# Hybrid encoder layer on one Trainium2 core: S5 tables set up behind the first input tiles, side lines a little later, row loads from GpSimd's queue, half of the last output blocks split ahead, and a dense copy of V

## The chip, the cores and the metric

The kernel runs on one core of a Trainium2 chip. Six sequencers work side by side and wait for each other through semaphores: PE (TensorE matmuls, with its weight loads shown as PEld), DVE (VectorE), ACT (ScalarE), POOL (GpSimd), and SP (SyncE), which here only issues DMAs. ACT and POOL issue some DMAs too. Each engine takes its instructions strictly in the order in which they stand. The metric is the device time in microseconds (us) of one execution.

## The reference

One layer of a streaming encoder, for 512 tokens of width 2048, all in fp32:

```python
mod = silu(c) @ w_ada + b_ada                        # six rows of 2048
h = layer_norm(x) * (1 + sc_m) + sh_m
u, q, k, v, z, beta, a, gate_s, gate_g = split(h @ w_in)
y_s = s5_mixer(u, ...) @ w_up_ssm                    # 64 groups, 16 channels, 64 states
y_g = gated_deltanet(q, k, v, z, beta, a, ...) @ w_up_gdn   # 8 heads, chunks of 64
y = (sigmoid(gate_s) * y_s + sigmoid(gate_g) * y_g) @ w_out
x = layer_norm(alpha * x + g_m * y, ln1_g, ln1_b)
h = layer_norm(x) * (1 + sc_f) + sh_f
x = layer_norm(alpha * x + g_f * swiglu(h), ln2_g, ln2_b)
```

The S5 mixer first turns its parameters (`lam_re`, `lam_im`, `log_dt`) into powers of a complex decay and an input factor (`fr`, `fi`); these tables don't depend on the tokens.

## The kernel before

**Products.** Every large product is made of three matmuls per 128x512 tile (`mm3`): the fp32 operands are split into a rounded part `hi` and a rest `lo`, and hi·hi, hi·lo and lo·hi are added in PSUM. These are called main matmuls here; there are 12,216 of them. The weights come as blocks of 512 KB (class `Weights`, L933): SP loads a block into one of three `raw` buffers, ACT casts it to `whi`, DVE subtracts to get `wlo`. `run_ahead` splits two blocks ahead of the one in use. A block serves 24 main matmuls in the input, gate and FFN products, and 12 in the w_mix product and in the last FFN output, where the roles are swapped.

**Stages.** 0 to 168 us: layer norm, adaLN (the 33.5 MB of `w_ada` that the first modulation needs pass through here in pieces) and the input tiles `u` of S5. To about 1061 us: the other input products, with the S5 and GDN work (eight batches, eight heads) set between the main matmuls. Then gates and merge to 1469, w_mix to 1683, and the FFN in six groups of eight hidden tiles, the last of four; the last group's output product and the final layer norm end the kernel.

**Order.** Class `Order` (L61 on) holds a model of the engines' clocks. Side work is written as generators ("lines"): `s5_setup`, `s5_line`, GDN's preparation and recurrence, adaLN, layer norm. Behind each main matmul `tick` (L132) gives a line its next step once `line.t + MARGIN` is not above the modelled clock of PE, where `line.t` is the modelled time at which the step's inputs are there. So MARGIN only moves where in each engine's order a step's instructions stand.

**S5.** `s5_setup` (L272) starts ahead of the input tiles: SP loads `lr`, `li`, `dt`; POOL computes exponentials and angles in 64x128 pieces, ACT takes `sn` and `cs`, POOL goes on to `ar`, `ai`, `fr`, `fi`, PE transposes these four into `px_s`, ACT copies them to `PAr`, `Pi`, `Ftab`, and POOL builds the tables. `o.drain(s5s)` forces the rest behind the input tiles. Each of the eight batches (`s5_batch`, L391) builds V on POOL, transposes it on PE into `G` (two ACT copies of 128x512), and uses V as the weights of eight matmuls into `pk`; these read V with a step of eight elements.

**w_mix and the end.** SP issues, beside the weight blocks, the rows of the modulation (`grow`, by `row_to`, L1598), the rows of the layer norm (`gg`, `gs`) and the tiles of `x` (`at<-in_x`). In the last FFN group the output weights are multiplied by the row `g_f` on DVE (`scaled`), so each block is first scaled, then cast and subtracted; there are eight blocks, two for each quarter `q` of the columns. `ws.limit` lets `run_ahead` split three of them; the other five are taken raw and split inside `last_parts` (L1787).

Of the kernel before, what the change touches and what calls it, by code (L numbers as in the profile page):

```python
# [11 lines left out]
F32 = mybir.dt.float32  # L12
# [44 lines left out]
class Order:  # L57
# [6 lines left out]
    MARGIN = 0.4  # L64
# [326 lines left out]
def s5_batch(k, j, prm, d_col):  # L391
# [56 lines left out]
    for half in range(2):  # L448
        pg = k.psum("s5")
        for i in range(4):  # L450
            pe.transpose(pg[:, 128 * i:128 * i + 128], V[:, 4 * half + i].rearrange("p h s -> p (h s)"), k.c(C_ID))
        act.copy(G[:, 4 * half:4 * half + 4].rearrange("p t n -> p (t n)"), pg)
    Kc = k.sm5.tile([128, 15, 16], F32, name="s5Kc", tag="s5Kc")
    pool.memset(Kc[:, 0:7], 0.0)
    for half in range(2):
        pk = k.psum("s5")
        for i in range(4):
            tau = 4 * half + i
            pe.matmul(pk[:, 128 * i:128 * i + 128], lhsT=V[:, :, :, 7 - tau].rearrange("p g h -> p (g h)"),
# [467 lines left out]

GATES_BEFORE = (0, 1, 1, 1, 1, 1, 1, 1)
# [4 lines left out]
class Weights:  # L933


    def __init__(self, k, pool):
        self.k, self.pool = k, pool
        self.specs, self.raw, self.parts, self.names = [], {}, {}, {}
# [17 lines left out]
    def split(self, upto):  # L956
        while self.cut < min(upto, len(self.specs) if self.limit is None else self.limit):
# [5 lines left out]
            if scale is not None:  # L963
                self.scaled(raw, kts, cols, scale)
            hi = self.pool.tile([128, WB], F32R, name="whi", tag="whi")
# [43 lines left out]
def kernel(ctx, tc, x, c, w_ada, b_ada, w_in, lam_re, lam_im, log_dt, b_re, b_im, c_re, c_im,  # L1009
# [73 lines left out]
    for hf in range(2):  # L1083
        for q in range(4):
            for c0 in range(0, 16, 2):
                ws.plan(w_mix[0, 128 * c0:128 * c0 + 256, 512 * q:512 * q + 512], 2, 512)
    groups = [(j0, min(HG, NHT - j0)) for j0 in range(0, NHT, HG)]
    ffn_order = []
    for gi, (j0, ng) in enumerate(groups):
        nh = min(NHALF, ng) if gi == 0 else 0  # L1090
        ffn_order.append([(j, [hf]) for hf in range(2) for j in range(nh)] + [(j, [0, 1]) for j in range(nh, ng)])
        for j, _ in ffn_order[-1]:
            for base in (0, HID):
                plan1(f_in[0, :, base + 128 * (j0 + j):base + 128 * (j0 + j) + 128])
        for q in range(4):
            for c0 in range(0, ng, 2):
                r0 = 128 * (j0 + c0)
                ws.plan(f_out[0, r0:r0 + 256, 512 * q:512 * q + 512], 2, 512, q if gi == len(groups) - 1 else None)
    ws.limit = len(ws.specs) - 5
# [71 lines left out]
    def ada_line(p, col0, pace):  # L1171
# [8 lines left out]
        depth = 3 if pace else 6 if deep else 4  # L1180
# [62 lines left out]
    start, set5 = ExitStack(), ExitStack()  # L1243
    sp = start.enter_context(pool_of(name="start", bufs=1, side="right"))
    s5p = set5.enter_context(pool_of(name="s5set", bufs=1))
# [116 lines left out]
    s5s = o.add(s5_setup(k, s5p, lam_re, lam_im, log_dt))  # L1362
# [32 lines left out]
    o.drain(s5s)  # L1395
    start.close()
    set5.close()
# [32 lines left out]
    k.sm5 = sp5 = sps.enter_context(pool_of(name="sp5", bufs=1))  # L1430
    alias5 = {"g": "X", "y": "S"}
    alias5w = {"G": "W", "H": "V", "R": "W"}
    k.t5 = lambda n: sp5.tile([128, 512], F32, name="s_" + n, tag="s" + alias5.get(n, n), bufs=2 if n == "U" else 1)
    k.t5w = lambda n: sp5.tile([128, 1024], F32, name="s_" + n, tag="s" + alias5w.get(n, n))
# [421 lines left out]
```

## Time and profile before

| | us |
|---|---|
| median of 3 runs | 3168.74 (3167.68 to 3170.12) |
| the profiled execution | 3170.34 |
| its span, first to last instruction | 3168.6 |
| PE busy in it | 3033.4 |
| mean granted TensorE clock | 0.977 of full speed |

A main matmul of 128x512 starts every 0.227 us at the full clock. Its record is longer, since matmuls overlap, so PE's busy time says when PE had work and not how fast it went; for that the granted clock stands beside it. A wait is named by the instruction that waited and by the one whose semaphore came last. Waits of engines other than PE cost time only where PE stands behind them.

### The profile page before, as it was taken

The numbers are of one execution on the slowest core, as the hardware profiler recorded it, in microseconds if no ns is written. First come the engines' busy times: TensorE is split into PE (matmuls) and PEld (weight loads), VectorE is DVE, ScalarE is ACT, GpSimd is POOL, SyncE is SP. The second block draws the span as 40 slices with busy tenths as digits, with TensorE's granted clock in tenths as the row PEclk, the third lists the DMA queues.
The fourth block names the chain that finished last, engine by engine and source line by source line (L and its number), as shares of the span: only waits on it lengthen the run. The fifth ranks groups of instructions, "written<-read, shape, count | busy, mean of one in ns | idle before, by whom it ended". The sixth has DMA issues, their size and how long they took to land.

```text
span 3168.6 us, 40305 instructions
## 1 busy us (share of the span) xinstructions
PE 3033.4 (96%) x15953; PEld 2499.7 (79%) x15953; DVE 1663.2 (52%) x2217; ACT 954.5 (30%) x1378; POOL 782.8 (25%) x832
## 2 busy tenths in 40 slices
PE   5899989989999999999989999999999999999997
PEld 2588878778777878888769998888888888888885
DVE  6647777666554576756687543333333333333337
ACT  3233333333222343323345631222222222222121
POOL 4834655455112255100022102002001100200202
PEclk8899989999999999999999999999999999999998
DMA  9654334333332688656866553333333333333333
GB/s 330 229 148 110 98 87 111 105 105 95 117 109 84 201 288 288 224 188 207 261 225 192 169 170 103 100 97 110 94 99 110 97 100 101 105 95 102 109 101 120
DMA packets 513534, 458.14 MB, mean 145 GB/s; under 512 B 56145, under 2 KB 403633, under 8 KB 513345
## 3 DMA queue, kind: packets, MB, share of 16 engines
q1 hardware_dynamic: 495904, 408.91, 42.4%
q0 software_dynamic: 10240, 33.56, 3.1%
q10 hardware_dynamic: 7200, 13.10, 1.2%
q8 instruction: 125, 2.05, 0.3%
q14 instruction: 65, 0.52, 0.1%
HBM read 435.60 MB, written 19.89 MB: 144 GB/s over the span
## 4 chain that ended last, share of the span: by engine, by line
PE 64%; DMA 4%; DVE 4%; issue 2%; ACT 2%; POOL 1%; SPq 0%; ACTq 0%; DVEq 0%; POOLq 0%
PE pm L211 47%; PE px_fo L211 14%; DMA raw<-in_w_mix_out_dram 2%; PE px_gd L211 2%; DVE wlo L170 1%; ACT whi L170 1%; DVE at L170 1%; DMA w<-in_w_ada_dram 1%; DVE aacc L170 1%; PE px_ada L211 0%; DMA raw<-in_ffn_w_in_dram 0%; PE px_s L211 0%; ACT f L170 0%; DVE bt L170 0%; DMA g_G<-dG 0%
## 5 line engine op out<-in xcount | busy, mean ns | idle before, releaser
L211 PE MATMUL pm<-at,whi 128*128 128x512 f32 (+1 forms) x3744 | 1145.5, 389 | 8.0 <-ACT whi L170 5.0
L170 DVE TENSOR_TENSOR wlo<-raw,whi 128x1024 fp32r<-128x1024 f32 x541 | 683.4, 1265 | 800.6 <-ACT whi L170 789.7
L170 ACT CAST whi<-raw 128x1024 fp32r<-128x1024 f32 x541 | 567.0, 1050 | 1066.4 <-PE pm L211 454.9
L211 PEld LDWEIGHTS pm<-at,whi 128*128 128x128 f32 x3744 | 683.7, 191 | 137.8 <-ACT whi L170 5.4
L211 PE MATMUL pm<-at,wlo 128*128 128x512 f32 (+1 forms) x1872 | 717.3, 383 | 2.6 <-DVE wlo L170 2.5
L211 PE MATMUL pm<-bt,whi 128*128 128x512 f32 (+1 forms) x2464 | 680.3, 362 | 0.0
L211 PEld LDWEIGHTS pm<-bt,whi 128*128 128x128 f32 x2464 | 442.2, 189 | 71.7 <-issue 0.5
L211 PE MATMUL pm<-bt,wlo 128*128 128x512 f32 (+1 forms) x1232 | 446.0, 362 | 1.5 <-DVE wlo L170 1.5
L211 PEld LDWEIGHTS pm<-at,wlo 128*128 128x128 f32 x1872 | 356.5, 190 | 72.9 <-DVE wlo L170 3.5
L170 POOL TENSOR_TENSOR at<-at,ld 128x512 f32<-128x512 f32 x80 | 120.5, 1538 | 1109.8 <-DVE ld L170 1109.8
L211 PE MATMUL px_fo<-whi,bt 128*128 128x512 f32 x960 | 298.8, 389 | 0.0
L211 PEld LDWEIGHTS pm<-bt,wlo 128*128 128x128 f32 x1232 | 232.9, 189 | 37.8 <-DVE wlo L170 2.2
L211 PEld LDWEIGHTS px_fo<-whi,bt 128*128 128x128 f32 x960 | 180.2, 188 | 37.5
L211 PE MATMUL px_fo<-wlo,bt 128*128 128x512 f32 x480 | 186.7, 389 | 0.0
L170 DVE SCALAR_TENSOR_TENSOR aacc<-w,ccol,aacc 128x512 f32<-128x512 f32 x176 | 163.8, 931 | 6.1 <-DMA w<-in_w_ada_dram 5.1
L170 POOL TENSOR_TENSOR rs<-rs,mhalf 128x1 f32<-128x1 f32 (+1 forms) x13 | 11.3, 872 | 453.1 <-DVE rs L170 453.1
L211 PE MATMUL pm<-whi,bt 128*128 128x512 f32 x336 | 112.5, 405 | 9.8 <-DVE at L170 9.8
L211 PE MATMUL px_fo<-whi,at 128*128 128x512 f32 x336 | 108.2, 392 | 2.0 <-ACT whi L170 2.0
L211 PEld LDWEIGHTS px_fo<-wlo,bt 128*128 128x128 f32 x480 | 90.1, 188 | 18.7
L170 DVE SCALAR_TENSOR_TENSOR gs<-gg,pm 128x512 f32<-128x512 f32 x36 | 24.7, 687 | 142.2 <-ACT gg L170 142.2
L170 DVE TENSOR_TENSOR gs<-gs,pm 128x512 f32<-128x512 f32 x36 | 24.7, 687 | 119.9 <-PE pm L211 119.9
L211 PEld LDWEIGHTS pm<-whi,bt 128*128 128x128 f32 x336 | 64.9, 193 | 26.4 <-DVE at L170 11.7
(412 smaller groups left out, 3232.4 us busy)
## 6 DMA issues: line engine op xcount, KB each, us to landing
raw<-in_ffn_w_in_dram SPq DMA_DIRECT2D x208, 512.0 KB, 4.1
raw<-in_w_in_dram SPq DMA_DIRECT2D x146, 512.0 KB, 4.3
raw<-in_ffn_w_out_dram SPq DMA_DIRECT2D x88, 512.0 KB, 3.7
wad<-in_w_ada_dram SPq DMA_DIRECT2D x64, 512.0 KB, 6.3
w<-in_w_ada_dram SPq DMA_DIRECT2D x128, 256.0 KB, 4.2
raw<-in_w_mix_out_dram SPq DMA_DIRECT2D x64, 512.0 KB, 5.3
w<-in_w_ada_dram POOLq DMA_DIRECT2D x91, 256.0 KB, 4.8
gg<-in_w_ada_dram POOLq DMA_DIRECT2D x37, 256.0 KB, 5.2
```

The costliest lines, as they stand in the source:

```text
L170: r = f(*a, **kw)
L211: r = self.e.matmul(out, **kw)
```

## The change

Six parts. (1) MARGIN is 1.0 us in place of 0.4 until the S5 and GDN lines are done, and 0.4 from there. (2) ACT copies V into a dense `Vs` (tile `s_K`) and the `pk` matmuls take their weights from it. (3) `s5_setup` is no line of its own ahead of the input tiles; it runs as the first part of the S5 line behind them, and the paced adaLN line keeps two loads in flight in place of three. (4) The rows and the tiles of `x` are loaded from POOL's queue. (5) In the last FFN group four of the eight output blocks are planned among the input blocks, two behind each of the first two hidden tiles, and split into spare tiles; one block in place of five is taken raw. (6) For this the four rows `g_f` are loaded as the group begins.

```diff
@@ -61,7 +61,7 @@
...
-    MARGIN = 0.4
+    MARGIN = 1.0
@@ -450,13 +450,15 @@
...
+    Vs = k.t5w("K")
+    act.copy(Vs.rearrange("p (s n) -> p s n", s=8), V.rearrange("p g h s -> p s (g h)"))
...
-            pe.matmul(pk[:, 128 * i:128 * i + 128], lhsT=V[:, :, :, 7 - tau].rearrange("p g h -> p (g h)"),
+            pe.matmul(pk[:, 128 * i:128 * i + 128], lhsT=Vs[:, 128 * (7 - tau):128 * (8 - tau)],
@@ -962,6 +967,15 @@
...
                 self.scaled(raw, kts, cols, scale)
+            if i in self.kept:
+                pairs = self.kept[i]()
+                for s, (hi, lo) in enumerate(pairs):
+                    r = raw[:, cols * s:cols * s + cols]
+                    self.k.act.copy(hi, r)
+                    self.k.v.tensor_tensor(out=lo, in0=r, in1=hi.bitcast(F32), op=S)
+                self.parts[i] = tuple(zip(*pairs))
+                self.cut += 1
+                continue
             hi = self.pool.tile([128, WB], F32R, name="whi", tag="whi")
@@ -1084,19 +1098,28 @@
...
+    kept = []
...
+        out_blocks = [(q, c0) for q in range(4) for c0 in range(0, ng, 2)]
+        def plan_out(n, scale=None):
+            for q, c0 in itertools.islice(out_blocks, n):
+                r0 = 128 * (j0 + c0)
+                ws.plan(f_out[0, r0:r0 + 256, 512 * q:512 * q + 512], 2, 512, q if scale else None)
+            del out_blocks[:n]
+        last = gi == len(groups) - 1
...
-        for q in range(4):
-            for c0 in range(0, ng, 2):
-                r0 = 128 * (j0 + c0)
-                ws.plan(f_out[0, r0:r0 + 256, 512 * q:512 * q + 512], 2, 512, q if gi == len(groups) - 1 else None)
-    ws.limit = len(ws.specs) - 5
+            if last and j < EARLY // 2:
+                kept += range(len(ws.specs), len(ws.specs) + 2)
+                plan_out(2, True)
+        plan_out(len(out_blocks), last)
+    ws.limit = len(ws.specs) - 1
@@ -1177,7 +1200,7 @@
...
-        depth = 3 if pace else 6 if deep else 4
+        depth = 2 if pace else 6 if deep else 4
@@ -1240,9 +1263,8 @@
...
-    start, set5 = ExitStack(), ExitStack()
+    start = ExitStack()
...
-    s5p = set5.enter_context(pool_of(name="s5set", bufs=1))
@@ -1359,7 +1381,6 @@
...
     ws.run_ahead()
-    s5s = o.add(s5_setup(k, s5p, lam_re, lam_im, log_dt))
     xnT = []
@@ -1392,9 +1413,7 @@
...
             ws.run_ahead()
-    o.drain(s5s)
     start.close()
-    set5.close()
@@ -1448,7 +1466,14 @@
...
         u_out(upsum[j])
-    s5l = o.add(s5_line(k, (b_re, b_im, c_re, c_im), dcol))
+    def s5_all():
+        with pool_of(name="s5set", bufs=1) as s5p:
+            yield from s5_setup(k, s5p, lam_re, lam_im, log_dt)
+        k.sm5 = sps.enter_context(pool_of(name="sp5", bufs=1))
+        yield from s5_line(k, (b_re, b_im, c_re, c_im), dcol)
+    s5l = o.add(s5_all())
     psb = [None]
@@ -1483,6 +1508,7 @@
...
+        o.MARGIN = 0.4
@@ -1596,7 +1622,7 @@
...
-        ld.dma_start(out=t, in_=bc(src[0:1, 512 * q:512 * q + 512], [128, 512]))
+        pool.dma_start(out=t, in_=bc(src[0:1, 512 * q:512 * q + 512], [128, 512]))
@@ -1639,7 +1665,7 @@
...
-                ld.dma_start(out=r, in_=bc(src[0:1, 512 * q:512 * q + 512], [128, 512]))
+                pool.dma_start(out=r, in_=bc(src[0:1, 512 * q:512 * q + 512], [128, 512]))
@@ -1698,7 +1724,7 @@
...
                         xa[t][q] = at(F32)
-                        ld.dma_start(out=xa[t][q], in_=x[0, 128 * t:128 * t + 128, sl])
+                        pool.dma_start(out=xa[t][q], in_=x[0, 128 * t:128 * t + 128, sl])
                     for i in range(2):
@@ -1762,11 +1788,21 @@
...
-            k.gf_rows = [row_to(t2("ld"), drow[5], q) for q in range(2)]
+            q2 = P2[1]
+            k.gf_rows = [row_to(t, drow[5], q) for q, t in enumerate(
+                (t2("ld"), t2("ld"), t2("grow"), q2.tile([128, 512], F32, name="gf3", tag="gf3", bufs=1)))]
+            spare = gsp[ng:] + [[adp.tile([128, 512], F32R, name="w1", tag="w1", bufs=4) for _ in range(2)] for _ in range(2)]
+            spare += [[adp.tile([128, 512], F32R, name=n, tag=n, bufs=1) for n in ("aacc", "go")],
+                      [q2.tile([128, 512], F32R, name=n, tag=n, bufs=1) for n in ("aacc2", "keep")]]
+            for n, i in enumerate(kept):
+                ws.kept[i] = lambda n=n: spare[2 * n:2 * n + 2]
+            early = []
...
+            if gi == len(groups) - 1 and j < EARLY // 2:
+                early += [ws.next(2, 512) for _ in range(2)]
@@ -1781,16 +1817,19 @@
-    k.gf_rows += [row_to(bt(F32), drow[5], q) for q in range(2, 4)]
     parts = []
...
             his, los = [], []
-            if q > 1:
-                yield k.gf_rows[q]
+            yield k.gf_rows[q]
             for c0 in range(0, ng, 2):
-                if 2 * q + c0 // 2 < 3:
+                n = 2 * q + c0 // 2
+                if n < EARLY:
+                    his += early[n][0]
+                    los += early[n][1]
+                    continue
+                if n < 7:
                     hi, lo = ws.next(2, 512)
```

PE in the first S5 batch before; `px_s<-cst,s_V` are the transposes of V, `px_s<-s5Cs,s_V` the `pk` matmuls, `pm` main matmuls.

```order
319 L211 MATMUL pm<-at,whi 128x512 x2
320 L211 MATMUL pm<-at,wlo 128x512
321 L216 MATMUL px_s_1656<-cst,s_V 128x128 x4
322 L216 MATMUL px_s_1662<-cst,s_V 128x128 x4
323 L211 MATMUL px_s_1670<-s5Cs,s_V 128x128 x4
324 L211 MATMUL pm<-at,whi 128x512 x2
325 L211 MATMUL pm<-at,wlo 128x512
326 L211 MATMUL px_s_1685<-s5Cs,s_V 128x128 x4
327 L211 MATMUL pm<-at,whi 128x512 x2
```

The same place after; `px_gd` is GDN's.

```order
598 L211 MATMUL pm<-at,whi 128x512 x2
599 L211 MATMUL pm<-at,wlo 128x512
600 L216 MATMUL px_s_2476<-cst,s_V 128x128 x4
601 L216 MATMUL px_s_2482<-cst,s_V 128x128 x4
602 L211 MATMUL px_s_2492<-s5Cs,s_K 128x128 x4
603 L211 MATMUL px_gd<-g_X,g_TT 64x64 x8
604 L211 MATMUL px_gd<-g_TT,g_X 64x64 x8
605 L216 MATMUL px_gd<-cst,g_E 128x128 x4
606 L211 MATMUL pm<-at,whi 128x512 x2
607 L211 MATMUL pm<-at,wlo 128x512
608 L211 MATMUL px_s_2541<-s5Cs,s_K 128x128 x4
```

The transposes and the first four `pk` matmuls stand next to each other in both; these four now read the copy. ACT at this place after:

```order
140 L170 COPY s_G<-px_s_2476 128x512
141 L170 COPY s_G<-px_s_2482 128x512
142 L170 COPY s_K<-s_V 128x1024
143 L170 COPY g_MT<-px_gd 128x512
144 L170 COPY s_S<-px_s_2573 64x256 x4
```

The copy `s_K<-s_V` stands behind both copies to `G`, which wait for the transposes.

ACT in the last FFN group before; `gg` is the gate of a hidden tile, `at<-gs` the cast of that tile's finished values, `whi` a weight block, two for each half of a hidden tile.

```order
947 L170 ACTIVATE gg<-pm 128x512
948 L170 CAST whi<-raw 128x1024 x2
949 L170 CAST at<-gs 128x512
950 L170 CAST whi<-raw 128x1024 x2
951 L170 ACTIVATE gg<-pm 128x512
952 L170 CAST whi<-raw 128x1024 x2
953 L170 CAST at<-gs 128x512
954 L170 CAST whi<-raw 128x1024 x2
```

The same place after; `bt`, `w`, `aacc` `<-raw` are casts of the early output blocks.

```order
957 L170 ACTIVATE gg<-pm 128x512
958 L170 CAST bt<-raw 128x512 x4
959 L170 CAST at<-gs 128x512
960 L170 CAST whi<-raw 128x1024 x4
961 L170 ACTIVATE gg<-pm 128x512
962 L170 CAST w_22917<-raw 128x512
963 L170 CAST w_22919<-raw 128x512
964 L170 CAST aacc<-raw 128x512
965 L170 CAST aacc_22923<-raw 128x512
966 L170 CAST at<-gs 128x512
967 L170 CAST whi<-raw 128x1024 x4
```

The two weight blocks that stood between `gg` and `at<-gs` have the early output blocks' casts in their place, and stand behind `at<-gs`.

POOL in the w_mix stage after; before, the DMAs among these rows stood on SP.

```order
682 L170 DMA at<-in_x_dram 128x512
683 L170 TENSOR_TENSOR rs<-rs,mhalf_137 128x1
684 L170 DMA gg<-in_ln_g_dram 128x512
685 L170 DMA gs<-in_ln_b_dram 128x512
686 L170 TENSOR_TENSOR at<-at,gg 128x512
687 L170 TENSOR_TENSOR at<-at,gs 128x512
688 L170 DMA grow<-dgm 128x512
689 L170 DMA at<-in_x_dram 128x512 x2
690 L170 DMA gg<-in_ln_g_dram 128x512
691 L170 DMA gs<-in_ln_b_dram 128x512
692 L170 TENSOR_TENSOR at<-at,gg 128x512
```

POOL's `at<-at,gg` takes a tile that ACT has written, and the loads for later quarters now stand behind it.

## Rows read from the trace of the kernel before

**Rows 1.** The page's part on busy time, and of the chain that ended last the line by engine, tile and line of the program (share of the span).
```profile
PE 3033.4 (96%) x15953; PEld 2499.7 (79%) x15953; DVE 1663.2 (52%) x2217; ACT 954.5 (30%) x1378; POOL 782.8 (25%) x832
...
PE pm L211 47%; PE px_fo L211 14%; DMA raw<-in_w_mix_out_dram 2%; PE px_gd L211 2%; DVE wlo L170 1%; ACT whi L170 1%; DVE at L170 1%; DMA w<-in_w_ada_dram 1%; DVE aacc L170 1%; PE px_ada L211 0%; DMA raw<-in_ffn_w_in_dram 0%; PE px_s L211 0%; ACT f L170 0%; DVE bt L170 0%; DMA g_G<-dG 0%
```
**Rows 2.** Table by stage: stretch in us and its length, then busy us (and instructions) of PE, PEld, DVE, ACT and POOL, the granted TensorE clock, the share of the DMA engines in use, GB/s.
```profile
60.00:88.00 28.00, 25.02 (x111) 16.32 (x110) 16.15 (x14) 9.87 (x15) 24.33 (x47) 0.94 0.95 326
88.00:134.00 46.00, 35.12 (x118) 20.76 (x117) 22.93 (x22) 11.29 (x19) 38.75 (x63) 0.80 0.69 233
134.00:168.00 34.00, 32.29 (x125) 19.92 (x124) 27.44 (x58) 11.40 (x16) 18.40 (x29) 0.90 0.56 186
...
400.00:600.00 200.00, 187.84 (x1340) 155.37 (x1340) 140.31 (x243) 67.13 (x139) 112.07 (x109) 0.95 0.35 95
...
1480.00:1690.00 210.00, 187.48 (x815) 148.93 (x814) 149.98 (x198) 88.27 (x109) 27.61 (x18) 0.96 0.73 235
...
3100.00:3121.00 21.00, 15.84 (x38) 9.60 (x38) 16.04 (x21) 6.74 (x11) 0.00 (x0) 0.67 0.51 177
```
**Rows 3.** Waits of PE in 88 to 134 us: instruction's tile and line, what it waited for, us in total, times, longest.
```profile
PE pm L211 <- ACT whi L170: 5.0, 1, 5.0
PE px_s L216 <- POOL fi L170: 2.6, 1, 2.6
PE pm L211 <- DVE wlo L170: 2.5, 1, 2.5
```
**Rows 4.** Waits of ACT in the same stretch, same columns.
```profile
ACT PAr L170 <- PE px_s L216: 12.5, 1, 12.5
...
ACT sn L170 <- POOL sr L170: 10.0, 1, 10.0
```
**Rows 5.** Timeline of POOL, first and last of the operations that lead from the loaded `dt` to the table entries `fi` (start us, duration us, instruction, idle before it and what ended that).
```profile
57.24 1.29 POOL L170 TENSOR_SCALAR er<-dt 64x1 f32<-64x1 f32 x1 [9.40 <-DMA dt<-in_ssm_log_dt_dram]
...
123.95 0.45 POOL L170 TENSOR_TENSOR fi<-t,den 64x128 f32<-64x128 f32 x1
```
**Rows 6.** Waits of PE in 200 to 1100 us, the first and the last of 14 kinds; over all 14 kinds they come to 37.8 us in 23 waits.
```profile
PE px_s L216 <- POOL s_V L170: 6.7, 4, 3.8
...
PE px_s L211 <- ACT s_G L170: 0.3, 1, 0.3
```
**Rows 7.** Table by stretch (columns as in rows 2) around one wait of PE for POOL `s_V`, which lasted from 724.27 to 726.43 us.
```profile
724.00:727.00 3.00, 0.83 (x6) 0.57 (x5) 2.93 (x3) 0.00 (x0) 2.51 (x2) 0.95 0.54 149
727.00:730.00 3.00, 3.00 (x16) 2.78 (x14) 0.00 (x0) 1.17 (x2) 0.00 (x0) 0.50 0.11 32
730.00:733.00 3.00, 3.00 (x42) 2.85 (x41) 2.05 (x4) 0.00 (x0) 0.00 (x0) 0.98 0.00 0
```
**Rows 8.** The instructions on tile `px_s`, weight loads of two kinds: durations min/median/max in ns, then first and last start.
```profile
L211 PEld LDWEIGHTS px_s<-s5Cs,s_V x128: 312/335/337, 218.0 to 733.3; 128*128 128x128 f32 x128
...
L211 PEld LDWEIGHTS px_s<-s_U,s_K x128: 186/192/192, 269.7 to 778.6; 128*128 128x128 f32 x128
```
**Rows 9.** Timeline of PE in the first of the eight S5 batches (columns as in rows 5, with the count of records; an fp32 matmul leaves two records).
```profile
217.22 1.09 PE L216 MATMUL px_s<-cst,s_V 128*128 128x128 f32 x8
218.15 2.07 PE L211 MATMUL px_s<-s5Cs,s_V 128*128 128x128 f32 x8
...
220.75 1.94 PE L211 MATMUL px_s<-s5Cs,s_V 128*128 128x128 f32 x8
```
**Rows 10.** Groups of ACT instructions in 188 to 1061 us: busy us, mean ns of one, idle before.
```profile
L170 ACT CAST whi<-raw 128x1024 fp32r<-128x1024 f32 x102 | 106.8, 1048 | 178.9 <-PE pm L211 146.3 <-issue 24.3 <-DVE wlo L170 3.1
L170 ACT COPY s_K<-s_R 128x1024 f32<-128x1024 f32 x8 | 17.6, 2201 | 0.1
...
L170 ACT COPY s_G<-px_s 128x512 f32<-128x512 f32 x16 | 8.8, 588 | 35.1 <-PE px_s L216 35.1
```
**Rows 11.** Waits of PE in 1480 to 1800 us.
```profile
PE pm L211 <- DVE wlo L170: 7.0, 9, 1.0
...
PE pm L211 <- ACT whi L170: 1.3, 1, 1.3
```
**Rows 12.** Waits of SP, the queue that issues the loads, in 1480 to 1720 us.
```profile
SPq L170 <- DVE wlo L170: 99.4, 54, 6.1
...
SPq L170 <- DVE bt L170: 6.4, 1, 6.4
```
**Rows 13.** Waits of POOL in the same stretch.
```profile
POOL at L170 <- ACT at L170: 26.9, 3, 14.2
```
**Rows 14.** The page's list of DMA issues, the same load from SP's queue and from POOL's (count, KB each, median us from issue to landing).
```profile
w<-in_w_ada_dram SPq DMA_DIRECT2D x128, 256.0 KB, 4.2
...
w<-in_w_ada_dram POOLq DMA_DIRECT2D x91, 256.0 KB, 4.8
```
**Rows 15.** Timeline around the start of the last output blocks.
```profile
3097.39 0.69 DVE L170 TENSOR_TENSOR gs<-gs,pm 128x512 f32<-128x512 f32 x1 [2.48 <-PE pm L211]
...
3098.11 0.62 ACT L170 CAST bt<-gs 128x512 fp32r<-128x512 f32 x1 [4.46 <-DVE gs L170]
...
3099.37 1.22 DVE L170 TENSOR_TENSOR raw<-raw,ld 128x1024 f32<-128x1024 f32 x1
...
3100.98 1.04 ACT L170 CAST whi<-raw 128x1024 fp32r<-128x1024 f32 x1 [2.25 <-DVE raw L170]
...
3102.08 0.55 PE L211 MATMUL px_fo<-whi,at 128*128 128x512 f32 x1 [2.00 <-ACT whi L170]
```

More of the change, by code (lines that the diff above doesn't have):

```diff
@@ L925 @@
 NHALF = 8
+EARLY = 4
 GATES_BEFORE = (0, 1, 1, 1, 1, 1, 1, 1)
@@ L937, in __init__ @@
         self.k, self.pool = k, pool
-        self.specs, self.raw, self.parts, self.names = [], {}, {}, {}
+        self.specs, self.raw, self.parts, self.names, self.kept = [], {}, {}, {}, {}
         self.used = self.loaded = self.cut = 0
@@ L1429 @@
     k.tc = lambda n: gp.tile([128, 256], F32, name="g_" + n, tag=n, bufs=1 if n == "X" else 2)
-    k.sm5 = sp5 = sps.enter_context(pool_of(name="sp5", bufs=1))
     alias5 = {"g": "X", "y": "S"}
     alias5w = {"G": "W", "H": "V", "R": "W"}
-    k.t5 = lambda n: sp5.tile([128, 512], F32, name="s_" + n, tag="s" + alias5.get(n, n), bufs=2 if n == "U" else 1)
-    k.t5w = lambda n: sp5.tile([128, 1024], F32, name="s_" + n, tag="s" + alias5w.get(n, n))
+    k.t5 = lambda n: k.sm5.tile([128, 512], F32, name="s_" + n, tag="s" + alias5.get(n, n), bufs=2 if n == "U" else 1)
+    k.t5w = lambda n: k.sm5.tile([128, 1024], F32, name="s_" + n, tag="s" + alias5w.get(n, n))
     k.u_done = 0
```

## The prediction

> **What bounds the kernel now.** I read the page's busy times first, then the chain that ended last, the table by stage, and the waits of PE in each stage. PE is busy for 3033.4 of 3168.6 us, and one kind of main matmul alone holds 47% of the chain [rows 1]; none of the six parts removes a main matmul. So the change can only win where PE stood still or ran at a low clock: the start, where PE is busy for 35 of 46 us at a granted clock of 0.80 [rows 2]; the S5 and GDN stage, with 37.8 us of waits [rows 6]; w_mix, with 187 of 210 us busy [rows 2]; and the last output blocks, with 15.8 of 21 us busy at 0.67 [rows 2]. The clock goes with the waits: PE waited 2.16 us until 726.43, from 727 to 730 the granted clock was 0.50, the lower of its two levels (1.2 in place of 2.4 GHz), and after that 0.98 [rows 7]. Half a clock over 3 us is 1.5 us lost, so a wait of over 2 us costs that much more than itself.
>
> **S5 set up behind the input tiles: -17 at the start.** From 88 to 168 us the DMA engines moved 46 us x 233 GB/s + 34 x 186 = 17.0 MB. From 60 to 88 they moved 326 GB/s at 0.95 of their time [rows 2]; at that rate 17.0 MB takes 52 us. If nothing else held these 80 us up, they would end 28 us earlier. That is the largest gain. The smallest is what names POOL's tables directly, the 2.6 us of `px_s <- POOL fi` [rows 3] and 1.5 of clock: about 4. Between lie 5.0 us for `whi` and 2.5 for `wlo` [rows 3], which I put down to ACT: it stood 10.0 us in front of `sn` and 12.5 in front of `PAr` [rows 4], weight casts queued behind both, and both are S5 instructions that go. I take 17, near the middle.
>
> **The same set-up in the middle: +4.** Its POOL operations from `dt` to `fi` took 124.40 - 57.24 = 67 us [rows 5]. After, 291 main matmuls stand between its first instruction and the transposes on PE that need `fi`, 291 x 0.227 = 66 us, in which POOL has GDN's work too and ACT again has `sn`, `cs` and `PAr` in a row with casts. If it just fits, it costs nothing. If ACT is blocked as before, PE loses 5.0 + 2.6 + 2.5 again [rows 3] and two times 1.5 of clock, 13 us. I take 4, nearer to the fit.
>
> **MARGIN: -13.** Each step of a line gets its place 0.6 us later on PE. The 23 waits of rows 6 come to 37.8 us; four or so are under 0.6 us and go whole, and 19 that shrink by about 0.55 us give 10. Those just over 2 us, like the one of rows 7, may then leave the clock up, 1.5 us each; I count two, 3 us. At best, with more falling under it, -20. At worst lines that end later hold their tiles longer and others wait instead: +5.
>
> **Dense V: +21.** A weight load from V takes 335 ns, one from a dense tile 192 [rows 8]. The two groups of four `pk` matmuls took 2.07 and 1.94 us, and eight dense records of the same shape 1.09 [rows 9]: 4.01 - 2.18 = 1.8 us saved in each batch. Against it stands a new wait. The first four `pk` matmuls stand directly behind the eight transposes, which end at 217.22 + 1.09 = 218.3 [rows 9]. They now need ACT's copy of V, which stands behind the two copies to `G`. Those wait for the transposes, the first for four of them (ready at about 217.9), and take 0.59 us each [rows 10], to 219.1. The copy itself isn't in the trace. ACT's dense 128x1024 took 1.05 us; `s_K <- s_R`, 128x1024 with a step of eight elements on one side, took 2.20 [rows 10]. The new copy reads with a step of eight, so it is nearest to the second: it ends at 221.3, PE waits 3.0 us, and loses 1.5 to the clock: 3.0 + 1.5 - 1.8 = 2.7 a batch, 8 x 2.7 = 21 us. At the dense price PE waits 1.9 us and keeps its clock, and the edit costs 8 x 0.1, nothing. It ends at -5 if main matmuls cover part of that, and at +25 if a cast of 1.05 us stands ahead on ACT in half of the batches.
>
> **Row loads from POOL: -7.** In w_mix PE waits 7.0 us for `wlo` and 1.3 for `whi` [rows 11], because blocks land late. SP, which loads them, also waits for tiles that the rows and `x` need, as the 6.4 us for `bt` [rows 12]; 99.4 us are for its own raw buffers, and stay [rows 12]. Without the others the blocks are asked for sooner. I count 7 of these 8.3; at best 12, with the clock; at worst +5, where `x` comes later. What hides a late `x`: it is issued at the third of a quarter's eight blocks and used behind the last, six blocks of 12 x 0.227 = 2.72 us later, 16 us, and a load from POOL's queue lands after 4.8 [rows 14].
>
> This is where the Trainium skill speaks against the change. The row shows 4.8 us from POOL's queue and 4.2 from SP's for one kind of load [rows 14], which is inside the 16 us. "SBUF — State Buffer", in the box on how DVE can hold up DMAs, says that descriptors of a DMA from GpSimd's queue are written by GpSimd, which DVE locks out during some of its operations, and that SP's or ACT's queue is the remedy. The row's 0.6 us doesn't show more than that; by the row the sum stays, by the rule the fourth rival below gains.
>
> **Last output blocks: -3.** In 3100 to 3121 us 38 matmuls took 21 us in place of 38 x 0.227 = 8.6 [rows 2]: 12.4 us lost, since five raw blocks are scaled (1.22), cast (1.04) and subtracted one behind the other [rows 15]. One raw block behind seven ready ones hides, so 12 go. But behind the first two hidden tiles of the group the next weight block's cast now stands behind `at <- gs`, which waits for the tile's own end: `gs` 0.69, the cast 0.62, the block's cast 1.04 [rows 15], and some 0.3 us of passing on, about 2.6, with 1.5 of clock and some 0.4 until `wlo` 4.5, twice 9. If the stall is as in rows 15, 2.00 us, and half of it is covered, the part gives -10; if the early blocks push DVE's `wlo` back too, +2. The rows `g_f` are issued a whole group ahead and hide.
>
> **Sum.** -17 + 4 - 13 + 21 - 7 - 3 = -15. The profiled execution took 3170.3, of which 3168.6 is the span; 3170.3 - 15 = 3155.3. It lay 1.6 us above the median of 3168.74, which gives 3153.7; I say **3154**.
>
> **Rivals.**
> *All gains, V free* (0.27): the copy costs the dense price, and the set-up fits. -17 - 13 + 0 - 7 - 3 = -40, so 3129; with the start at 22 and MARGIN at 18, 3119. For it: ACT is busy for 67 of 200 us in this stage [rows 2]. Against: the only copy of this size with a step took 2.20 [rows 10].
> *The start's loss is moved* (0.20): `fi` comes late and ACT blocks the casts as before, 13 in place of 4; MARGIN gives only its 5 us of small waits. -17 + 13 - 5 + 21 - 7 - 3 = +2, so 3171. For it: 67 us of POOL work against 66 of cover [rows 5]. Against: beside GDN's steps POOL no longer works against the adaLN sums on DVE, which were at work in those 67 us.
> *POOL's queue holds `x` up, slower* (0.13): POOL waits for ACT up to 14.2 us in one place [rows 13], and a load behind that wait is issued that much later. With 16 us of lead and 4.8 to land it begins to cost above 11 us. A lag of 20 us, two such waits in part, costs 9 us in each of four quarters, 36 in place of -7: 3154 + 43 = 3197; with half the quarters 3176. The rule on GpSimd's descriptors would work here. For it: loads now stand between POOL's `at<-at,gg`. Against: for the first two quarters nothing on POOL stands ahead of them.
> *The change as summed* (0.40): 3154, itself from 3140 to 3166.
>
> **Chances.** I call within 0.2% the same, 6.3 us, 3162.4 to 3175.1, about what a measurement of this kernel can tell from no change. Faster: 0.33 of the summed case's 0.40, all of the first rival's 0.27 and 0.05 of the second's, 0.65. Same: 0.07, 0.11 and 0.02 of the third's, 0.20. Slower: 0.04 of the second's and 0.11 of the third's, 0.15. The range takes most of the first rival and the third's low case: 3117 to 3178.
>
> **What would show it.** Start: the 216th main matmul, at 168 us before, near 150, and no wait for `fi` there. Set-up: PE waits for `px_s <- POOL fi` near 250 us of 0 to 4 us. V: eight waits of PE for ACT `s_K` of about 3 us with a granted clock of 0.50 behind; under 2 us each means the dense price. MARGIN: fewer than 19 waits in the stage, V's apart. w_mix: busy time of PE nearer to the stage's length, no PE wait for DVE `at` behind a late `x`. End: two PE waits of about 2.6 us for ACT `whi` in the last group, none over 1 us in the output blocks. The forecast is wrong if the copy of V takes under 1.5 us, if the middle shows waits for POOL's tables of over 5 us, or if w_mix gets longer.

## The result, and the profile after

The changed kernel takes 3131.78 us (median of 4 runs, 3128.48 to 3134.89) against 3168.21 of the kernel before; the ratio is 0.9884, 95% interval 0.9867 to 0.9902, so 36 us or 1.2% faster. The forecast was 3154, 15 us faster. The way was right and the time lay in the range (3117 to 3178), but the gain was 2.4 times the one forecast. The first rival's 3129 hits the time by luck: its reason, that the copy of V is free, is refuted by the runs. The profiled execution has a span of 3129.2 us and a clock of 0.982.

Where the time went is easiest seen between given main matmuls, since their number is the same in both. The starts of the k-th main matmul are counted in the two profiled executions; the table gives the us between them.

| main matmuls | stage | before | after | difference |
|---|---|---|---|---|
| 0 to 216 | input tiles of S5 | 98.4 | 80.3 | -18.1 |
| 216 to 294 | to the old place of the S5 line | 20.6 | 17.7 | -2.9 |
| 294 to 2931 | S5 and GDN | 920.5 | 909.0 | -11.5 |
| 2931 to 4464 | gates, merge | 360.0 | 356.1 | -3.9 |
| 4464 to 5232 | w_mix | 214.2 | 207.6 | -6.6 |
| 5232 to 6000 | first FFN tiles | 103.0 | 108.5 | +5.5 |
| 6000 to 11000 | FFN | 1051.4 | 1052.4 | +1.0 |
| 11000 to 12000 | to the last group | 226.7 | 235.2 | +8.5 |
| 12000 to the end | last outputs, layer norm | 104.0 | 95.0 | -9.0 |

Another 2.3 us lie ahead of the first main matmul, so these two executions differ by 39 us where the medians differ by 36.

The page's busy times after, as in rows 1:

```profile
PE 3003.2 (96%) x15953; PEld 2485.0 (79%) x15953; DVE 1648.4 (53%) x2217; ACT 971.5 (31%) x1386; POOL 814.8 (26%) x904
```

PE is busy for 30 us less, at the same share. The table by stage after, with columns as in rows 2; the last two stretches stand 40 us earlier than in rows 2, as the work does:

```profile
88.00:134.00 46.00, 46.00 (x166) 26.65 (x165) 32.80 (x34) 15.30 (x21) 0.00 (x0) 0.91 0.92 320
134.00:168.00 34.00, 34.00 (x156) 28.17 (x155) 13.28 (x15) 12.66 (x18) 0.00 (x0) 0.95 0.45 137
...
1440.00:1650.00 210.00, 192.64 (x855) 153.96 (x855) 156.90 (x208) 90.29 (x111) 47.48 (x52) 0.97 0.76 247
...
3060.00:3081.00 21.00, 21.00 (x94) 17.29 (x93) 14.64 (x18) 3.86 (x5) 1.15 (x3) 1.00 0.30 104
```

From 88 to 134 us PE is busy throughout at 0.91, and POOL not at all: its tables are gone from there [rows 2, 5]. The DMA engines move 320 GB/s in place of 233, and none of the waits of rows 3 is left. In the last outputs PE is busy for 21 of 21 us at 1.00, in place of 15.84 at 0.67.

Waits of PE from 170 to 1100 us, answering rows 6 (the first, the third and the sixth of ten kinds; the others come to 16.0 us):

```profile
PE px_s L211 <- ACT s_K L170: 21.5, 8, 2.7
...
PE px_s L216 <- POOL s_V L170: 4.8, 3, 2.5
...
PE px_s L216 <- POOL fi L170: 2.2, 1, 2.2
```

The eight waits for V's copy are there, 2.7 us each; that for `fi` in the middle is one of 2.2 us. Without those of `s_K` PE waits 23 us in place of 37.8. One batch, on the timeline, answering rows 9:

```profile
308.08 1.07 ACT L170 COPY s_G<-px_s 128x512 f32<-128x512 f32 x2 [5.14 <-PE px_s L216]
...
309.04 2.05 ACT L170 COPY s_K<-s_V 128x1024 f32<-128x1024 f32 x1
...
311.14 2.08 PE L211 MATMUL px_s<-s5Cs,s_K 128*128 128x128 f32 x8 [2.62 <-ACT s_K L170]
```

and the copy and the matmuls' weight loads by form (columns as in rows 8):

```profile
L211 PEld LDWEIGHTS px_s<-s5Cs,s_K x128: 186/192/338, 311.1 to 868.8; 128*128 128x128 f32 x128
...
L170 ACT COPY s_K<-s_V x8: 2035/2036/2066, 309.0 to 861.4; 128x1024 f32<-128x1024 f32 x8
```

The copy stands behind both `G` copies and takes 2.04 us; PE, done with the transposes at 308.51, waits 2.62. The weight loads fell from 335 to 192 ns, as a dense tile has it [rows 8].

The waits of PE at the end, from 2900 us on:

```profile
PE pm L211 <- ACT whi L170: 4.7, 2, 2.4
PE pm L211 <- DVE wlo L170: 1.1, 2, 0.5
```

Two waits for `whi`, 2.4 us the longer, stand where the early blocks' casts took the place of the next tile's, and the wait for `whi` of rows 15 is gone.

### The profile page after: what moved, and what is told of

Same layout as the page of the kernel before. It is cut to its first block, busy times and chain, and to the rows that moved or that the text cites. A ratio compares the mean times of both kernels' runs of the same rounds, so it can differ in the third digit from the quotient of the medians.

```text
span 3129.2 us, 40248 instructions
## 1 busy us (share of the span) xinstructions
PE 3003.2 (96%) x15953; PEld 2485.0 (79%) x15953; DVE 1648.4 (53%) x2217; ACT 971.5 (31%) x1386; POOL 814.8 (26%) x904
## 4 chain that ended last, share of the span: by engine, by line
PE 81%; POOL 6%; DVE 4%; DMA 3%; ACT 3%; issue 2%; SPq 0%; ACTq 0%; POOLq 0%; DVEq 0%
PE pm L211 57%; PE px_fo L211 15%; PE px_gd L211 3%; PE px_s L211 2%; DMA raw<-in_w_mix_out_dram 2%; DVE wlo L170 1%; PE px_adr L211 1%; ACT whi L170 1%; PE px_u L211 1%; PE px_ada L211 1%; POOL s_V L170 1%; DVE at L170 1%; POOL eq L170 1%; DVE aacc L170 1%; POOL g_E L170 0%
## 5 line engine op out<-in xcount | busy, mean ns | idle before, releaser
L211 PEld LDWEIGHTS px_fo<-whi,bt 128*128 128x128 f32 x960 | 180.2, 188 | 37.4
L170 POOL DMA_DIRECT2D w<-in_w_ada_dram x101 | 55.4, 550 | 91.8 <-DVE aacc L170 65.4
```

What stands on the lines that cost most here:

```text
L170: r = f(*a, **kw)
L211: r = self.e.matmul(out, **kw)
```

## The experiments

All were timed beside the kernel before, which read 3168.2 to 3169.1 throughout. Differences under some 4 us between two changed kernels say little. Up to main matmul 2931 the changed kernel and three of its variants below (loads from SP, the old tail, the early blocks between) have the same instructions in the same order on PE, DVE, ACT and POOL, and their profiled executions took 909.0 to 913.1 us from 294 to 2931.

**Undoing one part at a time.** First the copy of V:

```diff
-    Vs = k.t5w("K")
-    act.copy(Vs.rearrange("p (s n) -> p s n", s=8), V.rearrange("p g h s -> p s (g h)"))
...
-    lhsT=Vs[:, 128 * (7 - tau):128 * (8 - tau)]
+    lhsT=V[:, :, :, 7 - tau].rearrange("p g h -> p (g h)")
```

> The changed kernel with one part undone: the pk matmuls read V itself again and ACT makes no copy. Theory A (the prediction's term): the copy costs 21 us over the eight batches, so without it the time falls from 3132 to about 3111. Theory B (accounts of the trace after: 21.5 us of waits for s_K, about 7 us of half clock behind them, less 15 us of faster matmuls): it costs 13, so about 3119. Rival C: the copy pays, because PE's stops there only take the place of other stops: 3135 or more, with the waits for other engines in the S5 and GDN stage grown by 15 us or more.

It took 3113.75 us, ratio 0.9827 (0.9814 to 0.9841): 18 us faster without the copy. Theory A's 21 is nearest. Between 294 and 2931 9 us went (909.0 to 899.8; up to 13 by the spread just named), the rest in w_mix (4) and the first FFN tiles (7), where only the order differs. Rival C falls.

MARGIN back to 0.4:

```diff
-    MARGIN = 1.0
+    MARGIN = 0.4
```

> The changed kernel with MARGIN 0.4 throughout. Theory A (the prediction's term): MARGIN is worth 13 us, so about 3145. Theory B (accounts of the trace after: waits other than for s_K fell from 38 to 23 us, and half clock behind them by about 6): 21 to 23 us, so about 3154, with the waits in the stage back near 38 us beside s_K's. Rival C: MARGIN is worth nothing and the side work only had to start later: 3132.

3155.79 us, ratio 0.9962 (0.9950 to 0.9975): 24 us slower. The stretch 294 to 2931 rose to 941.3 us with 60 us of stops, 37 of them not for `s_K`. (The profiled execution, 3164 us, is the slowest of five, the others 3152 to 3157, so its stages read high.) Theory B holds, A is too small, C falls.

The S5 set-up at the start again:

```diff
+    s5s = o.add(s5_setup(k, s5p, lam_re, lam_im, log_dt))
     xnT = []
...
+    o.drain(s5s)
     start.close()
...
-        depth = 2 if pace else 6 if deep else 4
+        depth = 3 if pace else 6 if deep else 4
```

> The changed kernel with the S5 set-up back ahead of the input tiles and the paced adaLN line at three loads. Theory B: the start gained 20 us and the set-up in the middle costs one wait of 2.2 us, so about 3150, and the 216th main matmul comes at 168 us in place of 148. Theory A (the prediction's terms): 17 less 4, 3145. Rival C: the start's gain is given back in the middle by lines that begin later: 3132, with the 2931st main matmul 0 to 3 us from where it is now.

3150.84 us, ratio 0.9944 (0.9930 to 0.9957): 19 us slower. 0 to 216 took 99.4 us again, and 294 to 2931 911.2, within 2 us of the changed kernel's. So the start's gain isn't given back; B holds. The run puts back the set-up and the third load in flight together, so what each of them gave isn't told apart.

The loads from SP's queue again:

```diff
-        pool.dma_start(out=t, in_=bc(src[0:1, 512 * q:512 * q + 512], [128, 512]))
+        ld.dma_start(out=t, in_=bc(src[0:1, 512 * q:512 * q + 512], [128, 512]))
```

(and the same for the layer norm's rows and `x`).

> The changed kernel with the rows and the tiles of x loaded from SP's queue again. Theory A (the prediction's term): the loads from POOL are worth 7 us, so about 3139. Theory B (accounts of the trace after): w_mix gained 7 us and the first FFN tiles lost 7, since rows of the layer norm stand behind POOL's waits; together nothing, so 3130 to 3134, with main matmuls 4464 to 5232 about 7 us slower and 5500 to 6000 about 6 us faster than now. Rival C: the first FFN tiles are slower for another reason (the new order): the loss at 5500 to 6000 stays and the time is near 3139.

3126.19 us, ratio 0.9867 (0.9853 to 0.9880): 6 us faster. None of the three theories said this. w_mix fell from 207.6 to 201.6 us and the first FFN tiles stayed slow (109.3), so the loss there has another reason than POOL's queue, and the loads from POOL cost in w_mix what they were to bring. Behind the last matmul, in the final layer norm, another 3 us went (19.6 to 16.7). Both recur: in the seven kernels here with the loads on POOL's queue w_mix took 203.5 to 210.1 us, in the four changed kernels with them on SP's 200.2 to 201.6, and behind the last matmul these four took 16.7 or 16.8. PE's waits for weight blocks in w_mix, in the changed kernel:

```profile
PE pm L211 <- DVE wlo L170: 3.6, 4, 1.3
PE pm L211 <- ACT whi L170: 2.2, 1, 2.2
```

and with SP's queue, where none for `whi` is left:

```profile
PE pm L211 <- DVE wlo L170: 1.5, 3, 0.8
```

These are 4.3 of the 6 us. The first row of ACT's waits there, in the same two kernels:

```profile
ACT whi L170 <- DMA raw<-in_w_mix_out_dram: 64.8, 28, 9.3
```

```profile
ACT whi L170 <- DMA raw<-in_w_mix_out_dram: 53.0, 24, 4.3
```

With the rows on POOL's queue ACT waited up to 9.3 us for one weight block, with them on SP's up to 4.3. The sum of these waits is not the cost: in the kernel with three edits below, with SP's queue, it is 65.1 us, and w_mix takes 200.2.

The old tail:

```diff
-EARLY = 4
+EARLY = 0
...
-    ws.limit = len(ws.specs) - 1
+    ws.limit = len(ws.specs) - 5
```

> The changed kernel with no output block split early and five taken raw, as before. Prediction's terms (12 us gained in the output blocks, 9 lost in front): 3 us slower, 3135. Accounts of the trace after (9 us gained behind main matmul 12000, 8.5 lost from 11000 to 12000): 3132, the same. Rival: the early part is a clear gain or loss of 5 us or more.

3137.24 us, ratio 0.9901 (0.9886 to 0.9916): 5.5 us slower. 11000 to 12000 went back to 226.7 us and the stretch behind to 105.8, so by its own two stretches the early part gains 2.3 us; most of the rest lies between 294 and 2931 (913.1), which this edit doesn't touch. It is a small gain, near the 3 us of the prediction's terms.

**MARGIN alone, in the kernel before.** This was the run that settled the case:

```diff
-    MARGIN = 0.4
+    MARGIN = 1.0
...
         o.drain(gl)
+        o.MARGIN = 0.4
```

> The kernel before with one part alone: MARGIN 1.0 until the S5 and GDN lines are done. Prediction's term: -13, so 3155. Theory (its worth is the 24 us that undoing it cost in the changed kernel): 3144, with the stops of PE between main matmuls 294 and 2931 at 15 to 23 us in place of 37.5. Rival: it is worth that much only beside the copy of V, whose waits it gives room: 3158 to 3165.

3132.25 us, ratio 0.9882 (0.9865 to 0.9898): 37 us faster, as much as the whole change. Every expectation put the gain too low. Three other values followed:

> The kernel before with MARGIN 0.7 until the S5 and GDN lines are done. Theory M (a step that is placed later finds its inputs there; the stops shrink with the margin and so does the half clock behind them): between 0.4 and 1.0, main matmuls 294 to 2931 in 900 to 912 us, stops there 24 to 33 us, time 3145 to 3158. Rival J (each margin gives another order, and the order decides by chance): the stretch lies outside 895 to 918, or the stages with the same margin in both (gates, w_mix, first FFN tiles) differ from before by more than 8 us in sum and make up most of the difference.

> The kernel before with MARGIN 1.6 until the S5 and GDN lines are done. Theory M: most of the 13 stops that are left at 1.0 are chains that are late by over 1 us, so a little more: stops 10 to 17 us, main matmuls 294 to 2931 in 880 to 889 us, time 3122 to 3132. Rival L (steps that wait longer end the lines later and hold tiles, so other waits grow): the stretch is 892 us or more. Rival J (chance of the order): the stretch is near 890 and the later stages decide, by up to 10 us either way.

> The kernel before with MARGIN 0.1 until the S5 and GDN lines are done, 0.4 behind them. Theory M (the steps are placed too early for what DVE, ACT and POOL really take, so an earlier place makes long waits): main matmuls 294 to 2931 take 930 us or more, 9 or more waits of PE of at least 2 us, time 3175 to 3195. Rival J (0.4 happened to give a bad order, and any other margin gives a better one): the stretch at 895 to 912 us, 3145 to 3160. Rival N (the margin matters only up from 0.4): 915 to 925 us and 3163 to 3173.

| MARGIN | us | ratio, 95% interval | 294 to 2931 | PE's stops there | 2931 to 4464 | w_mix | first FFN tiles |
|---|---|---|---|---|---|---|---|
| 0.1 | 3153.25 | 0.9950 (0.9937 to 0.9962) | 921.0 | 37.4 | 355.5 | 207.0 | 102.6 |
| 0.4 (before) | 3168.7 | 1 | 920.5 | 37.5 | 360.0 | 214.2 | 103.0 |
| 0.7 | 3144.22 | 0.9916 (0.9901 to 0.9931) | 899.0 | 26.2 | 356.0 | 210.0 | 105.0 |
| 1.0 | 3132.25 | 0.9882 (0.9865 to 0.9898) | 889.7 | 19.0 | 356.4 | 206.9 | 107.2 |
| 1.6 | 3131.31 | 0.9879 (0.9865 to 0.9894) | 871.5 | 12.3 | 370.0 | 208.5 | 112.2 |

(Stops are waits of PE over 0.2 us, summed.) At 0.7 and 1.6 theory M is right on the stops and, to about 1 us, on the time; the stretch came out shorter than it said. At 0.1 M falls; rival N has the stretch right and rival J the time.

Two effects stand apart. In the S5 and GDN stretch a larger margin helps from 0.4 up, in PE's stops and in the busy time behind them; at 0.1 it is as at 0.4. (At 1.6 some line steps pass into the next stretch; the two together take 1241.5 us, against 1246.1 at 1.0 and 1280.5 at 0.4.) Behind it, where the margin is 0.4 in all five, the kernel before is slower than the others by 4 to 7 us in w_mix and, but for 1.6, by some 4 us in the gates: its order was a poor one there, and the four other margins are rid of it. For 0.1 this is 12 of its 15 us. The waits of PE show where, in the kernel before in the gates and in w_mix:

```profile
PE px_ada L211 <- DVE aacc L170: 2.7, 1, 2.7
```

```profile
PE px_ada L211 <- DVE aacc L170: 4.8, 1, 4.8
```

These are steps of the adaLN line; at 0.1 and 1.0 neither wait is there. The changed kernel at 0.4 has the first again (2.65 us, 360.7 us in the gates), so that one is no accident of a single kernel. The S5 and GDN stretch in the kernel before and at 1.0 (columns as in rows 2):

```profile
188.73:1109.23 920.50, 882.47 (x5896) 729.95 (x5894) 576.99 (x933) 301.69 (x574) 392.65 (x410) 0.97 0.40 114
```

```profile
188.11:1077.83 889.72, 870.39 (x5887) 721.37 (x5886) 563.13 (x921) 296.01 (x568) 380.28 (x395) 0.99 0.40 114
```

PE is busy for 12 us less with the same main matmuls; the granted clock rose from 0.97 to 0.99.

**Mending what cost.** The copy of V ahead of the transposes, with a step between:

```diff
+    Vs = k.t5w("K")
+    act.copy(Vs.rearrange("p (s n) -> p s n", s=8), V.rearrange("p g h s -> p s (g h)"))
     G = k.t5w("G").rearrange("p (t n) -> p t n", t=8)
...
     pool.memset(Kc[:, 0:7], 0.0)
+    yield G
```

> The changed kernel with ACT's copy of V put ahead of the transposes and their two copies, and a step of the line between these and the pk matmuls, so that main matmuls can stand between. Theory B (the wait for the copy is what costs, the dense weights themselves save): the eight waits for s_K go, 21.5 us and about 7 of half clock, so the stretch from main matmul 294 to 2931 falls from 909 to about 880 us and the time to about 3103, below the 3114 without any copy. Rival C (most of what the undone copy gave came from other places that only moved with the planner's order: 9 of 18 us were in that stretch): the stretch falls to 885 to 895 and the time ends between 3105 and 3120. Rival D: ACT now holds weight casts up for the copy's 2.0 us, and PE waits for whi instead: 3125 or more.

3096.84 us, ratio 0.9774 (0.9759 to 0.9788). The stretch took 878.8 us and has no wait for `s_K` left; its table row:

```profile
164.49:1043.28 878.79, 854.04 (x5892) 706.02 (x5890) 560.31 (x947) 310.15 (x576) 444.56 (x523) 0.99 0.40 113
```

B holds: the wait was the cost, and 30 of the 35 us lie in this stretch. Dense weights, with the copy off PE's path, are 17 us better than none. The added step of the line is part of that, since the kernel without a copy hasn't got it; what the step alone would give wasn't run. The prediction's price for the faster weight loads, 1.8 us a batch, accounts for 15.

The early output blocks between the blocks of the second product:

```diff
+                    if u and ws.used in ws.kept:
+                        early.append(ws.next(2, 512))
                     hi, lo = ws.next(8, 128)
```

> The changed kernel with each early output block planned between the blocks of the second product of a hidden tile in place of two behind the tile, so that the next tile's first weight blocks are cast ahead of at<-gs. Theory (the order of ACT's casts makes the stall): the two waits for whi of 2.4 us go, main matmuls 11000 to 12000 take 227 to 228 us in place of 235, and the time falls by 8, to about 3124. Rival (DVE, which now scales and subtracts blocks in between, is what is late): PE waits for wlo instead, the stretch stays at 232 or more and the time at 3130.

3127.37 us, ratio 0.9870 (0.9855 to 0.9884): 4 us faster. 11000 to 12000 took 227.4 us with no wait of PE, as the theory has it; the time fell by half of that. Between 294 and 2931, which the edit doesn't touch, the profiled execution took 912.2 us for 909.0, so the medians can't tell 4 from 8.

**Together.**

> The changed kernel with three edits that each were faster alone: the copy of V first (-35), rows and x from SP's queue (-6), the early output blocks between the blocks of a product (-4). If they add up, 3132 - 45 = 3087; if the order of the later stages decides again by chance, 3080 to 3097. A rival: with V's waits gone SP's queue is fuller in w_mix and the rows cost there again, 3097 or more.

3080.18 us, ratio 0.9722 (0.9708 to 0.9736): 88 us faster than before, 52 than the change. The sum of the three was 3087.

> The same three edits with MARGIN 1.6 in place of 1.0. Theory M: stops between main matmuls 294 and 2931 fall further, by 5 to 10 us with their clock, so 3077 to 3084 if the three edits alone give 3087. Rival L: lines that end later make other waits, 3090 or more.

3082.73, ratio 0.9729 (0.9715 to 0.9742): no gain over 1.0. The stretch took 876.2 us against 878.2, and its stops fell by 2 us and not by 5 to 10, so theory M falls here.

> The best kernel so far (three edits, 3080) with MARGIN kept at 1.0 to the end. Theory M: the lines of the layer norm and of adaLN beside w_mix and the first FFN tiles are placed too early too, their stops of 13.4 and 6.5 us shrink by a third or more, 3066 to 3075. Rival: there the lines are the longer chain, or the stops come from weight blocks, and a later place costs: 3080 or more.

3088.37, ratio 0.9742 (0.9728 to 0.9755): 8 us slower; the rival holds. Behind the S5 and GDN stage setting MARGIN back is right: the three stages there took 5 us more in sum, the first FFN tiles 114.0 us in place of 109.1.

## Why the prediction was right or wrong

| step, as forecast | forecast | by undoing it | else |
|---|---|---|---|
| S5 set up behind the input tiles, with its cost in the middle | -13 | -19 | |
| MARGIN | -13 | -24 | -37 alone |
| dense V | +21 | +18 | |
| row loads from POOL | -7 | +6 | |
| last output blocks | -3 | -5.5 | |

With MARGIN at what it gives alone the parts sum to -19.1 - 36.6 + 18.0 + 5.6 - 5.5 = -37.6, and the change measured -36.4; with the value from undoing it they sum to -25.0. The first sum mixes terms from two kernels, so its fit doesn't prove that the parts add up. By the profiled executions MARGIN gave the S5 and GDN stretch 31 us alone and 32 beside the other parts, and w_mix 7.3 and 2.5; undoing it cost 33 us between these executions and 24 between the medians, so much of the 12 us between 24 and 37 may be the spread of the runs.

**MARGIN is the step that failed.** It said that the 23 waits shrink by up to 0.6 us each, 10 us, with 3 for the clock, and it put the stages behind at nothing. Of the 21 us that the forecast missed, this term is 11 by undoing it and 24 by MARGIN alone; the next largest, the row loads, missed 13 the other way. In the stretch alone it gave 31: PE's stops fell by 18.5 and its busy time by 12. The working took each wait for a lateness that a shift shortens by at most the shift. Redone wait by wait from the trace of the kernel before, where eight of the 23 waits are under 0.6 us and not four, that gives at most 11.6 us for 0.6 and 6.5 for 0.3; the runs gave 18.5 at 1.0 and 11.3 at 0.7. At 0.1 the stops come to the same as at 0.4. So the waits aren't the old ones less the shift; each margin makes another set:

| MARGIN | stops of 2 us or more | us | shorter stops | us |
|---|---|---|---|---|
| 0.1 | 5 | 20.0 | 21 | 17.3 |
| 0.4 (before) | 9 | 29.1 | 12 | 8.4 |
| 0.7 | 2 | 5.8 | 21 | 20.3 |
| 1.0 | 5 | 12.7 | 10 | 6.3 |
| 1.6 | 2 | 6.9 | 5 | 5.4 |

From 0.4 to 1.0, 16.4 of the 18.5 us are of the long stops. The busy time fell with them, as the granted clock rose from 0.97 to 0.99. None of the three signs of being wrong that the prediction named appeared, and its sign for MARGIN, fewer than 19 waits beside V's, came true with 12: it counted waits and could not show a gain that was too small. One long stop followed back shows how several queues make it. Here is the longest, in the kernel before (columns as in rows 5):

```profile
668.46 2.49 POOL L170 TENSOR_TENSOR s_W<-PAi,s5Cs 128x1024 f32<-128x1024 f32 x1
...
668.99 2.44 DVE L170 TENSOR_TENSOR s_K<-s_S,tab81s 128x448 f32<-128x448 f32 x1
...
671.02 2.66 POOL L170 TENSOR_TENSOR s_H<-s_H,s_W 128x1024 f32<-128x1024 f32 x1
...
671.46 4.32 DVE L170 TENSOR_TENSOR s_S<-s_S,s_K 128x448 f32<-128x448 f32 x2
...
678.02 1.22 DVE L170 TENSOR_TENSOR wlo<-raw,whi 128x1024 fp32r<-128x1024 f32 x1
679.15 0.69 DVE L170 TENSOR_TENSOR g_v<-g_v,ro 128x512 f32<-128x512 f32 x1
...
679.98 1.09 PE L216 MATMUL px_gd<-cst,g_v 128*128 128x128 f32 x4 [5.19 <-DVE g_v L170]
```

PE waited 5.19 us for `g_v`, which stood on DVE behind S5's steps and a `wlo`. One of those steps took 2.44 us beside POOL's `s_W`, the next two 4.32 us together beside its `s_H` and GDN's `g_G`; the planner's model counts 0.67 us for each (0.2 + 448 x 0.00105, in `Engine`). At 1.0 there is no wait of PE for `g_v` in the stretch. The margin doesn't take such growth away: summed over the stretch, DVE's instructions took 105 us more in the kernel before than each at its fastest (the shortest of the same instruction and shape in the five kernels of the first table of margins), and 101 us more at 1.0. That fits a margin that leaves room for work which takes longer than the model has it. It is argued from this stop; the other stops were not followed.

Another 11 us of MARGIN weren't in the working at all: 3.6 in the gates and 7.3 in w_mix, where the margin didn't change. The table of margins shows that the order before was a poor one there. The first FFN tiles gave 4 back, where PE's waits for ACT `ld` rose from 2.4 to 7.2 us.

**The start** was sized about right, 17 forecast and 21 seen to matmul 294, and nothing was given back in the middle, where I had put 4: one wait of 2.2 us, after which the clock stayed up. On POOL the way from `dt` to `fi` took 57.5 us there in place of 67 [rows 5]. The second rival falls by the run with the set-up at the start.

**Dense V** was right in its wait: 2.7 us for 3.0, a copy of 2.04 us for the 2.20 taken from the row nearest to it. It was not right in the clock, which I had counted as falling behind all eight waits: it fell behind three, was down already ahead of two, behind a wait for `s_V`, and stayed at 1.00 in three. In its own stretch the part cost 9 to 13 us and not 21, as undoing it left PE other waits (30 us in place of 23). That the 18 in all comes near 21 is partly luck, since 11 of it lie in w_mix and the first FFN tiles, where only the order moved.

**Row loads** had the wrong sign. I put SP's waits for `bt` down to the rows and `x` [rows 12]; with these on POOL they were 9.0 us, and 8.8 with them on SP, so they are of other loads. The 7 us that I took for the gain in w_mix came with another margin alone. What the move did cost shows in PE's waits for weight blocks; why these come later is open. The landing times don't settle it: from POOL's queue `x` took 5.5 us in the median of 14 loads, but of SP's loads of `x` the traces hold one landing in the kernel with SP's queue (4.5) and four in the kernel before (7.3). So no run here shows whether the mechanism of the Trainium skill that I weighed ("SBUF — State Buffer", the box on how DVE can hold up DMAs) was at work; its advice, to issue from SP's or ACT's queue, agrees with the 6 us. The third rival's mechanism, `x` held up behind POOL's waits (the prediction calls it the fourth where it speaks of the rule), would cost at the end of a quarter; PE's waits for DVE `at` were 7.7 us with POOL's queue and 9.2 with SP's, so it was not what cost.

**The tail** had both halves right in kind: 8.5 lost of 9 forecast in front, 9 of 12 gained behind by the result, 11 by undoing it.

## What to carry to other kernels

In a kernel whose side work is placed by a planner, a placing constant is worth a sweep before anything is explained: values on both sides tell its own effect (here from 0.4 up, 31 us in its stage) from a poor order that every other value tried left behind (here some 10 us). Don't size such a constant by shortening each wait by the shift: another value makes another set of waits, and here the long ones, with the half clock behind them, gave most of the gain. And a copy that saves PE time costs it all back if it stands in an engine's queue behind what PE has just finished: put where its input is ready, with one more step of the line behind it, the same copy went from 18 us lost to 17 won.

## What the runs showed of the hardware

Two-input DVE instructions beside two-input POOL instructions on large tiles took more than four times as long: in the kernel before the products `s_K <- s_S` of 128x448 took 0.61 us in all seven cases without a POOL instruction beside them, 2.44 beside `s_W`, as the last fence shows, and up to 2.82 beside `s_H`. The same wait of PE doesn't always cost the clock: of the eight waits for `s_K` of 2.6 to 2.7 us in the changed kernel, two began with the clock already at 0.50, behind three it fell to a mean of 0.61 to 0.69 over the next 3.5 us, and behind three it stayed at 1.00. An ACT copy of 128x1024 that reads with a step of eight elements took 2.04 us, twice the 1.05 of a dense cast of that size [rows 10].
